# A mixing projection of eight block rows rewritten as seven block products, in a decoder block on one Trainium2 core

## The chip, the cores and the metric

One core of one Trainium2 chip runs the whole kernel in one launch. The metric is device time in microseconds (us), lower is better. Engines are named as in the profile: PE (matrix products; PEld is its weight load), DVE (vector), ACT (scalar), POOL (GpSimd), SP (the queue that issues nearly all DMAs).

## The reference, cut to what matters

```python
...
merged = jax.nn.sigmoid(z_ga) * y_attn + jax.nn.sigmoid(z_gc) * y_conv
x = x + rms_norm(merged @ w_mix_out[l], g_post_mix[l])
h = rms_norm(x, g_pre_ffn[l])
x = x + rms_norm(swiglu_ffn(h, w_ffn_in[l], w_ffn_out[l]), g_post_ffn[l])
```

Everything is float32; the change concerns `merged @ w_mix_out` and the norms behind it. `merged` has 1024 tokens by 1024 channels and `w_mix_out` is 1024 by 1024. `y_attn` and `y_conv` come from the attention and convolution branches ahead of this.

## The kernel before, in words

**Numbers.** Every float32 factor of a product is split into a high and a low part (type fp32r), and a product takes three matmuls: high·high, high·low, low·high. A split of 512 columns is one ACT cast (the high part) and one subtraction on DVE or POOL (the low part). One matmul is 128 rows by 128 columns by 512.

**Order.** All is unrolled and every engine runs its instructions in the order in which the program lists them (`manual_schedule`, line 71). Background work is a generator: `bg` (111) puts it in a list, and `tick` (121), called after every few matmuls, runs each generator one step further; `yield n` skips n ticks; `finish` (156) runs one to its end at once. So what a generator issues stands, on each engine, between the instructions that the main loop issues around that tick. SBUF has 42 tiles of 128x1024 (`slot`, line 80), 11 of 128x512 (`half`) and 3 of 128x1024 (`ring`). `B.weights(i)` (262) hands out weight tile i in split form, and has the loads and splits of the next ones issued ahead.

**The attention output projection** (1627 to 1643): for each n of 8, two units of 12 matmuls (n: 128 channels; unit: half of the tokens), then two DVE operations that multiply by a gate and add the convolution branch (1635, 1636; both have 128x512), an ACT cast (1638) and a DVE subtraction (1641): the split `merged`, transposed, in 16 tiles `mop`. POOL takes half of the weights' low parts (`wsplit`, 1626).

**The mixing projection** (1659 to 1687): tokens in tiles of 128, first two together and then one after another. For a tile, 8 channel blocks by 3 matmuls by 2 halves of the output columns accumulate into two PSUM banks (1671); 384 matmuls in all. All eight split weights stay in SBUF.

**The norms** (`mix_norm`, 1384, through `residual`, 1365) are the background of the next tile's matmuls. For one tile: two ACT squares with a sum, 128x512 from PSUM (1370); `rstd_rows` (1352), one ACT square root and five DVE operations on one column; two DVE products with gain and 1/root (1377); two DVE additions of x (1381); the store of the sum `x2` (1388). Then the second norm: an ACT square of 128x1024 (1392), `rstd_rows` again, an ACT scaling of 128x1024 to `hn` (1394). After the fourth tile of a half, 8 times four PE transposes of 128x128 (1402), an ACT scaling from PSUM (1408) and a split (1404; `split` is 1259, its ACT cast 1262, its DVE subtraction 1263): the tokens' half of `h2`, the FFN's input.

**The FFN** begins (1726 to 1738) with two columns j for the first token half, which need `h2[0]`; then the last tile's norm is finished and the same is done for the second half. Each unit calls `tick` 8 times. The norm of tile 7 and the transposes of `h2[1]` run as background of the first half. The FFN's output product (1931 to 1980) already is a product of seven block products in the form that the change gives the mixing projection.

Of the kernel before, what the change touches and what calls it, by code (L numbers as in the profile page):

```python
# [27 lines left out]
RMS_EPS = 1e-6  # L28

ROOT = 1 / 32  # L30
# [28 lines left out]
def f(ap):  # L59
    return ap.bitcast(F32)  # L60


class Build:
# [1298 lines left out]
        nc.vector.tensor_tensor(r, r, t, op=OP.mult)  # L1362
        return r

    def residual(self, banks, x, gain, out, gap=0):

        nc = self.nc
        ss = self.tiny(4, "ss", 4)
        for nh in range(2):
            nc.scalar.activation(out[:, nh * H:(nh + 1) * H], banks[nh], AF.Square, scale=ROOT, accum_out=ss[:, nh:nh + 1])  # L1370
        yield gap
        nc.vector.tensor_scalar(ss[:, 2:3], ss[:, 0:1], RMS_EPS, None, op0=OP.add)
        r = self.rstd_rows(ss[:, 1:2], ss[:, 2:3])
        yield gap
        for nh in range(2):
            s = slice(nh * H, (nh + 1) * H)
            nc.vector.scalar_tensor_tensor(out[:, s], banks[nh], r, gain[:, s], op0=OP.mult, op1=OP.mult)
            yield gap
        for nh in range(2):
            s = slice(nh * H, (nh + 1) * H)  # L1380
            nc.vector.tensor_tensor(out[:, s], out[:, s], x[nh], op=OP.add)
            yield gap

    def mix_norm(self, tt, banks, x):
        nc = self.nc
        x2 = self.ring()
        yield from self.residual(banks, x, self.g_mix, x2)
        nc.sync.dma_start(self.d_x2[tt], x2)
        yield 1
        hn = self.slot()  # L1390
        ss = self.tiny(4, "ss", 4)
        nc.scalar.activation(hn, x2, AF.Square, scale=ROOT, accum_out=ss[:, 0:1])
        r = self.rstd_rows(ss[:, 0:1], self.eps_rms)
        nc.scalar.activation(hn, x2, AF.Copy, scale=r)
        self.hn[tt // 4].append(hn)
        if tt % 4 == 3:
            yield 8
            op, y = [], None
            for kt in range(8):
                ps = self.bank("s")  # L1400
                for i in range(4):
                    nc.tensor.transpose(ps[:, i * 128:(i + 1) * 128], self.hn[tt // 4][i][:, kt * 128:(kt + 1) * 128], self.ident)
# [5 lines left out]
                nc.scalar.activation(y, ps, AF.Copy, scale=self.col(C_PREF + kt))  # L1408
                self.h2f[tt // 4].append(y)
                yield 1  # L1410
            op.append(self.split(y, H))
            self.h2[tt // 4] = op
            self.hn[tt // 4] = None

    def row_gain(self, src):
        g = self.slot()
# [4 lines left out]
def build(ctx, tc, aps):  # L1421
# [5 lines left out]
    def job(src, n=1024, kind=""):  # L1427
        J.append((src, n, kind))
        return len(J) - 1
# [18 lines left out]
    mx = [job(aps["w_mx"][j]) for j in range(8)]  # L1448
# [138 lines left out]
    def gate_load(d, late=0):  # L1587
        c = B.slot()
        if late:
            B.later(late, lambda: nc.sync.dma_start(c, d))  # L1590
        else:
            nc.sync.dma_start(c, d)
        return c

    nxt = gate_load(B.d_gc[0], 1)
    ws = {}
# [22 lines left out]
        B.finish(e)  # L1619
    if B.tags["g"] == 2:  # L1620
        B.banks(g=6, s=2)
    mop = [[None] * 8, [None] * 8]

    rest = lambda: None
    B.PIECE = 1
    B.wsplit = nc.gpsimd
    for n in range(8):

        B.ahead = int(n >= 5)
        w = B.weights(ao[n])  # L1630
        (c, y), nxt = nxt, (gate_load(B.d_ga[n + 1]), gate_load(B.d_gc[n + 1])) if n < 7 else None
        for hf in range(2):
            s = slice(hf * H, (hf + 1) * H)
            ps = B.unit(w, lambda kt: tuple(x[:, s] for x in B.OT[kt]), 4)
            nc.vector.tensor_tensor(c[:, s], ps, c[:, s], op=OP.mult)
            nc.vector.tensor_tensor(c[:, s], c[:, s], y[:, s], op=OP.add)
# [5 lines left out]
    y = None  # L1642
    rest()
    B.OT = None

    W = [B.weights(mx[0])]
    B.g_mix = B.row_gain(aps["g_mix_row"])
    B.hn, B.h2, B.h2f = [[], []], [None, None], [[], []]
    norms = []
# [7 lines left out]
    B.PIECE = 2  # L1657
    xt = {0: load_x(0), 1: load_x(1)}
    for tiles in ((0, 1), (2,), (3,), (4,), (5,), (6,), (7,)):
        banks = {tt: (B.bank(), B.bank()) for tt in tiles}  # L1660
        for kt in range(KT):
            if len(W) == kt:
                B.ahead = int(kt < KT - 1)
                W.append(B.weights(mx[kt]))
            for tt in tiles:
                m = mop[tt // 4]
                o = (tt % 4) * 128
                for st, wt, a, b in ((m[kt][:, o:o + 128], W[kt][0], 1, 0), (m[kt][:, o:o + 128], W[kt][1], 0, 0),
                                     (m[kt][:, H + o:H + o + 128], W[kt][0], 0, 1)):
                    for nh in range(2):  # L1670
                        nc.tensor.matmul(banks[tt][nh], st, wt[:, nh * H:(nh + 1) * H], start=bool(kt == 0 and a),  # L1671
                                         stop=bool(kt == KT - 1 and b))
                B.tick()
                B.tick()
            if tiles[0] == 7:
                W[kt] = None
        B.PIECE = 3
        B.ahead = 0
        m = None
        for tt in tiles:  # L1680
            if tt % 4 == 3:
                mop[tt // 4] = None
            if tt < 6:
                xt[tt + 2] = load_x(tt + 2)
            for e in norms[:-1]:
                B.finish(e)
            norms.append(B.bg(B.mix_norm(tt, banks[tt], xt.pop(tt))))
    for e in norms[:-1]:
        B.finish(e)


    B.PIECE = 4
    held = {}
# [38 lines left out]
    B.g_mix = None  # L1732
# [22 lines left out]


    NP = FT // 2
    ORDER = (("A11", "B11"), ("A12", "B21"), ("S2", "T2"), ("S1", "T1"), ("S4", "B22"), ("S3", "T3"), ("A22", "T4"))
    wo = aps["w_fo"]
    Wo, al, ws, T2, T3 = {}, {}, {}, {}, {}  # L1760
    L, R = slice(0, H), slice(H, T)

    def w_load(p, r, c):
        if (p, r) not in Wo:
# [293 lines left out]
```

## Time and profile before

| | us |
|---|---|
| median of 3 runs (lowest, highest) | 1708.28 (1707.19, 1709.27) |
| span of the profiled execution, first to last instruction | 1704.7 |
| median above that span | 3.6 |
| PE busy | 1686.8 (99%) |
| DVE, ACT, POOL busy | 1260.4 (74%), 800.6 (47%), 499.0 (29%) |
| mixing projection, first to last matmul issue | 969.1 to 1060.1 |

The profiled execution has no time of its own beside its span; the 3.6 us that the median has above it stand for what lies around the span. A row of instruction groups has: line, engine, operation, out<-in, shape, count | busy us, mean ns of one | idle time ahead of it and what ended it. A row of a timeline has: start us, duration us (of several merged ones, from the first's start to the last's end), engine, line, operation, out<-in, count [idle ahead <- what ended it]. A row of windows has: stretch, its length, then busy us and count for each engine, the granted clock, the DMA share and GB/s. Matmuls overlap in the pipeline: one lasts 0.39 us, but they follow each other faster.

### The profile page before, as it was taken

What the parts mean: (1) busy time and instruction counts of PE and PEld (TensorE: products, weight loads), DVE (VectorE), ACT (ScalarE), POOL (GpSimd) and SP (SyncE); (2) the same over time, 40 slices, a digit from 0 to 9 for tenths busy, and PEclk for the clock granted to TensorE, in tenths of its full rate; (3) what the DMA queues carried; (4) which work ended last, traced back from release to release, by engine and by line L of the source; (5) the groups of instructions that cost most, each with busy time, mean ns of one, the idle gap of its engine ahead of it and who ended that gap; (6) DMA issues with size and microseconds to landing.
All of it is one profiled execution on the core that took longest, in us unless ns stands there. A gap on an engine that the chain in (4) does not pass through costs nothing.

```text
span 1704.7 us, 23850 instructions
## 1 busy us (share of the span) xinstructions
PE 1686.8 (99%) x8374; PEld 1417.7 (83%) x8374; DVE 1260.4 (74%) x2216; ACT 800.6 (47%) x1574; POOL 499.0 (29%) x397
## 2 busy tenths in 40 slices
PE   8999999999999999999999999999999999999998
PEld 7788888888888889999888888888888888888886
DVE  6789988888999767777885845675565556677686
ACT  6344344434444576777712436633333333354463
POOL 0017777887886254655300310000000000000000
PEclk9999999999999999999999999999999999999999
DMA  4252433455567887778998722133223322494234
GB/s 166 104 185 87 149 124 130 152 196 177 173 167 176 269 266 211 222 218 224 311 290 294 254 74 88 68 111 112 93 93 112 111 93 93 155 376 137 102 133 155
DMA packets 162357, 283.39 MB, mean 166 GB/s; under 512 B 47249, under 2 KB 78732, under 8 KB 162236
## 3 DMA queue, kind: packets, MB, share of 16 engines
q1 hardware_dynamic: 161516, 281.18, 51.2%
q8 instruction: 66, 1.08, 0.3%
q0 software_dynamic: 432, 0.42, 0.1%
q14 instruction: 55, 0.45, 0.1%
q10 hardware_dynamic: 288, 0.27, 0.0%
HBM read 191.10 MB, written 95.42 MB: 168 GB/s over the span
## 4 chain that ended last, share of the span: by engine, by line
PE 94%; DMA 2%; ACT 1%; POOL 1%; issue 1%; DVE 1%; SPq 0%; DVEq 0%; ACTq 0%; POOLq 0%
PE p L334 15%; PE p L335 15%; PE p L336 15%; PE p L1942 12%; PE p L961 5%; PE p L1671 5%; PE p L318 5%; PE p L320 5%; PE p L319 5%; PE p L1142 3%; PE p L962 2%; PE p L1069 2%; PE p L569 2%; PE p L1107 2%; DMA b<-dk 1%
## 5 line engine op out<-in xcount | busy, mean ns | idle before, releaser
L334 PE MATMUL p<-b,b 128*128 128x512 f32 x1204 | 469.3, 390 | 0.5 <-ACT c L353 0.3
L335 PE MATMUL p<-b,b 128*128 128x512 f32 x1204 | 469.0, 389 | 0.0
L336 PE MATMUL p<-b,b 128*128 128x512 f32 x1204 | 468.9, 389 | 0.0
L334 PEld LDWEIGHTS p<-b,b 128*128 128x128 f32 x1204 | 226.1, 188 | 48.5 <-DVE c L853 1.0
L336 PEld LDWEIGHTS p<-b,b 128*128 128x128 f32 x1204 | 226.0, 188 | 47.0
L335 PEld LDWEIGHTS p<-b,b 128*128 128x128 f32 x1204 | 226.1, 188 | 46.8
L1942 PE MATMUL p<-b,b 128*128 128x512 f32 x924 | 209.6, 389 | 0.0
L1942 PEld LDWEIGHTS p<-b,b 128*128 128x128 f32 x924 | 173.5, 188 | 35.9
L699 DVE SCALAR_TENSOR_TENSOR p<-b,par,p 128x511 f32<-128x511 f32 (+14 forms) x232 | 163.3, 738 | 0.0
L318 PE MATMUL p<-b,b 128*128 128x512 f32 x368 | 147.3, 400 | 0.0
L961 PE MATMUL p<-b,b 128*128 128x512 f32 x384 | 145.0, 410 | 0.0
L320 PE MATMUL p<-b,b 128*128 128x512 f32 x368 | 143.8, 391 | 0.0
L319 PE MATMUL p<-b,b 128*128 128x512 f32 x368 | 143.6, 390 | 0.0
L208 ACT CAST b<-d 128x1024 fp32r<-128x1024 f32 x86 | 90.4, 1051 | 105.2 <-POOL d L229 55.1
L209 POOL TENSOR_TENSOR b<-d,b 128x1024 fp32r<-128x1024 f32 x44 | 106.9, 2430 | 79.9 <-ACT b L208 72.5
L209 DVE TENSOR_TENSOR b<-d,b 128x1024 fp32r<-128x1024 f32 x42 | 51.3, 1221 | 101.0 <-ACT b L208 101.0
L1263 DVE TENSOR_TENSOR b<-b,b 128x512 fp32r<-128x512 f32 x133 | 92.0, 696 | 23.2 <-ACT b L1262 21.2
L962 PE MATMUL p<-b,b 128*128 128x256 f32 x384 | 107.7, 281 | 0.0
L1262 ACT CAST b<-b 128x512 fp32r<-128x512 f32 x133 | 82.1, 619 | 47.6 <-PE p L1942 18.4
L1671 PE MATMUL p<-b,b 128*128 128x512 f32 x384 | 89.4, 392 | 0.0
L1082 ACT ACTIVATE c<-c,stat 128x128 f32<-128x128 f32 (+1 forms) x192 | 85.1, 447 | 6.7 <-DVE stat L1072 6.6
L208 ACT CAST b<-b 128x1024 fp32r<-128x1024 f32 x47 | 49.5, 1052 | 78.7 <-POOL b L236 37.2
(234 smaller groups left out, 2910.5 us busy)
## 6 DMA issues: line engine op xcount, KB each, us to landing
b<-w_in SPq DMA_DIRECT2D x30, 512.0 KB, 4.8
dk<-c SPq DMA_DIRECT2D x48, 256.0 KB, 3.0
dq<-c SPq DMA_DIRECT2D x48, 256.0 KB, 3.6
b<-dq SPq DMA_DIRECT2D x48, 256.0 KB, 3.9
b<-dk SPq DMA_DIRECT2D x48, 256.0 KB, 7.1
b<-w_fi SPq DMA_DIRECT2D x24, 512.0 KB, 4.7
d<-w_in SPq DMA_DIRECT2D x23, 512.0 KB, 4.1
dqS<-c SPq DMA_DIRECT2D x44, 256.0 KB, 2.1
```

What stands on the lines that cost most here:

```text
L209: self.wsplit.tensor_tensor(lo, x, f(hi), op=OP.subtract)
L318: nc.tensor.matmul(ps, hi[:, s], a, start=kt == 0, stop=False)
L319: nc.tensor.matmul(ps, hi[:, s], b, start=False, stop=False)
L320: nc.tensor.matmul(ps, lo[:, s], a, start=False, stop=kt == nk - 1)
L334: nc.tensor.matmul(ps, hi[:, s], a, start=first and kt == 0, stop=False, skip_group_check=True)
L335: nc.tensor.matmul(ps, hi[:, s], b, start=False, stop=False, skip_group_check=True)
L336: nc.tensor.matmul(ps, lo[:, s], a, start=False, stop=kt == 3, skip_group_check=True)
L699: nc.vector.scalar_tensor_tensor(A[i][:, j:], src[i][:, :H - j], w[i], A[i][:, j:], op0=OP.mult, op1=OP.add)
L961: nc.tensor.matmul(ps, a, w, start=kt == 0, stop=kt == KT - 1, skip_group_check=True)
L962: nc.tensor.matmul(ps[:, 256:], b, w[:, :256], start=False, stop=kt == KT - 1, skip_group_check=True)
L1671: nc.tensor.matmul(banks[tt][nh], st, wt[:, nh * H:(nh + 1) * H], start=bool(kt == 0 and a), stop=bool(kt == KT - 1 and b))
L1942: nc.tensor.matmul(acc[t], x, y, start=first and e == 0, stop=last and e == 2, skip_group_check=True)
```

## The change

The product `merged @ w_mix_out` is cut into 2 by 2 blocks on each side (token half and channel half; channel half and output half) and computed by seven block products in place of eight, with sums of blocks ahead of them and sums of results behind them (Winograd's form of Strassen's scheme). A block product is 4 channel blocks (p) by 4 token tiles (t) by 3 matmuls; each result has four PSUM banks, one for each t; the banks of X and Y are accumulated over several products and copied to SBUF in between (`C`).

- The weights `w_mx` are no longer split jobs: each is loaded whole (`Wm`) in the attention output projection's loop, one for each n.
- `merged` stays unsplit (`M`). `parts` issues, five steps ahead of the matmuls, the operands of step k (28 steps: 7 products by 4 p): `merged_part` (cast, DVE split, DVE sums) and `mixing_part` (ACT cast, POOL split, POOL sums).
- The order is A11·B11, A12·B21, S2·T2, S1·T1, S4·B22, S3·T3, A22·T4. Of the first token half the right output columns end in the fifth product, of the second half in the sixth and the left ones in the seventh.
- The sum of squares is made in two halves of the columns (`part_norm`), a half each time that one is complete; the gain is multiplied there too. `mix_norm` then has the rest. In the fifth product t is the outer loop, and each token tile's norm starts as that tile ends. The last two products alternate by token tile.

```diff
+    ORDER = (("A11", "B11"), ("A12", "B21"), ("S2", "T2"), ("S1", "T1"), ("S4", "B22"), ("S3", "T3"), ("A22", "T4"))
+    def merged_part(k):
...
+        al[k] = B.split(x, H)
+        if name == "A11":
+            add(half_of(S3, p), a[:, L], a[:, R], op=OP.subtract)
+        elif name == "A12":
+            add(a[:, R], a[:, R], b[:, R], op=OP.add)
+            add(a[:, L], a[:, R], a[:, L], op=OP.subtract)
+            add(b[:, L], b[:, L], a[:, L], op=OP.subtract)
...
+    def mixing_part(k):
+        sub = nc.gpsimd.tensor_tensor
...
+        if name == "T2":
+            sub(x, Wm[p, 1][:, R], Wm[p, 0][:, L], op=OP.subtract)
+        s = B.slot(F32R)
+        nc.scalar.copy(s[:, L], x)
+        sub(s[:, R], x, f(s[:, L]), op=OP.subtract)
...
+        if name == "B21":
+            sub(y[:, L], y[:, R], y[:, L], op=OP.subtract)
+        elif name == "T1":
+            sub(half_of(T2, p), Wm[p, 1][:, L], half_of(T2, p), op=OP.subtract)
+        elif name == "B22":
+            sub(T3[p][:, R], Wm.pop((p, 1))[:, R], T3[p][:, R], op=OP.subtract)
...
     for n in range(8):
+        Wm[p, r] = B.slot()
+        nc.sync.dma_start(Wm[p, r], aps["w_mx"][2 * p + r])
...
-            x = B.slot(F32R)
-            nc.scalar.copy(x[:, :H], c[:, s])
-            mop[hf][n] = x
-            rest()
-            rest = lambda x=x, c=c[:, s]: nc.vector.tensor_tensor(x[:, H:], c, f(x[:, :H]), op=OP.subtract)
+        M[n] = c
+        if n % 2 and n > 1:
+            parts(n // 2)
...
+    def part_norm(h, t, c, src):
+        nc.scalar.activation(B.junk(), src, AF.Square, scale=ROOT, accum_out=SM[h][t][:, c:c + 1])
+        nc.vector.tensor_tensor(o, src, B.g_mix[:, (L, R)[c]], op=OP.mult)
...
+    parts(4)
+    for i in range(4):
...
+        for p in range(NM):
+            for t in range(4):
+                mm(acc[t], t, k, p == 0 and i in (0, 1, 3), p == NM - 1)
+                if t == 0:
+                    parts(k + 5)
+        if i == 0:
+            for t in range(4):
+                nc.scalar.copy(C[0][t][:, L], X[t])
+        elif i == 1:
+            bg.append(B.bg(left0(Y)))
...
+    for t in range(4):
+        for p in range(NM):
+            mm(Y[t], t, k, False, p == NM - 1)
+            if p == 0:
+                parts(k + 5 + t)
+        nc.vector.tensor_tensor(o, Y[t], o, op=OP.add)
+        part_norm(0, t, 1, o)
+        for e in norms[:-1]:
+            B.finish(e)
+        norms.append(B.bg(tile_norm(0, t, 1)))
...
+    parts(7 * NM)
+    for i, t in ((5, 0), (5, 1), (6, 0), (5, 2), (6, 1), (5, 3), (6, 2), (6, 3)):
+        for p in range(NM):
+            mm(X[t], t, i * NM + p, False, p == NM - 1)
+        if i == 5:
+            nc.vector.tensor_tensor(o, X[t], o, op=OP.add)
+            part_norm(1, t, 1, o)
+        else:
+            part_norm(1, t, 0, X[t])
+            for e in norms[:-1]:
+                B.finish(e)
+            norms.append(B.bg(tile_norm(1, t, 0)))
```

In the diff the first loop over p runs the first four products (i from 0 to 3; `left0` adds and `part_norm`s the first half's left columns), the loop over t the fifth, and the list of pairs (i, t) the last two: i = 5 completes the second half's right columns, i = 6 its left ones and with them the tile.

In `mix_norm` two DVE operations (product with 1/root, sum with x, in one) take the place of the four at lines 1377 and 1381; its steps are: nothing, `rstd_rows`, the two DVE operations and the store, one tick skipped, the second norm, and for the fourth tile of a half eight ticks skipped ahead of the transposes.

More of the change, by code (lines that the diff above doesn't have):

```diff
@@ L1363, in rstd_rows, with junk, mix_norm @@
         return r
-    def residual(self, banks, x, gain, out, gap=0):
+    def junk(self):
+        return self.half()
+    def mix_norm(self, h, t, C, sums, c, x):
         nc = self.nc
[L1368 to L1374, printed above, removed]
+        yield 0
+        o, C[t] = C[t], None
+        r = self.rstd_rows(sums[:, c:c + 1], sums[:, 2:3])
+        yield 0
+        x2 = self.ring()
         for nh in range(2):
             s = slice(nh * H, (nh + 1) * H)
[L1377 to L1387, printed above, removed]
+            nc.vector.scalar_tensor_tensor(x2[:, s], o[:, s], r, x[nh], op0=OP.mult, op1=OP.add)
+        tt = 4 * h + t
         nc.sync.dma_start(self.d_x2[tt], x2)
+        o = x = None
         yield 1
@@ L1624, in build, with parts @@
+    done = 0
+    def parts(upto):
+        nonlocal done
+        while done < min(upto, 7 * NM):
+            merged_part(done)
+            mixing_part(done)
+            done += 1
     rest = lambda: None
@@ L1626, in build @@
     B.wsplit = nc.gpsimd
+    B.banks(g=6, s=2)
     for n in range(8):
@@ L1655, in load_x @@
         return x
[L1657 to L1684, printed above, removed]
@@ new lines, in tile_norm, with left0, mm @@
+    def tile_norm(h, t, c):
+        yield from B.mix_norm(h, t, C[h], SM[h][t], c, xt.pop(4 * h + t))
+    def left0(Y):
+        for t in range(4):
+            o = C[0][t][:, L]
+            nc.vector.tensor_tensor(o, Y[t], o, op=OP.add)
+            part_norm(0, t, 0, o)
+            first_half(0, t, 0)
+            yield 2
+    def mm(bank, t, k, first, last):
+        a, w = al[k], ws[k]
+        h, l = a[:, t * 128:(t + 1) * 128], a[:, H + t * 128:H + (t + 1) * 128]
+        for x, y, e in ((h, w[:, L], 0), (h, w[:, R], 1), (l, w[:, L], 2)):
+            nc.tensor.matmul(bank, x, y, start=first and e == 0, stop=last and e == 2, skip_group_check=True)
+        B.tick()
@@ L1685, in build @@
             for e in norms[:-1]:
                 B.finish(e)
-            norms.append(B.bg(B.mix_norm(tt, banks[tt], xt.pop(tt))))
+            norms.append(B.bg(tile_norm(1, t, 0)))
+            if t < 2:
+                xt[6 + t] = load_x(6 + t)
+        if t == 3:
+            for p in range(NM):
+                del al[i * NM + p], ws[i * NM + p]
+    o = X = None
     for e in norms[:-1]:
@@ L1757, in build @@
     NP = FT // 2
[L1758 removed]
     wo = aps["w_fo"]
[L1760 to L1761 removed]
+    Wo, T2, T3 = {}, {}, {}
     def w_load(p, r, c):
```

94 lines of the change are left out of this document (81 added, 13 removed).

## The prediction, made before the result was known

> **What bounds the kernel now.** First the page's head and three rows of its instruction groups:
>
> ```profile
> PE 1686.8 (99%) x8374; PEld 1417.7 (83%) x8374; DVE 1260.4 (74%) x2216; ACT 800.6 (47%) x1574; POOL 499.0 (29%) x397
> ...
> L1942 PE MATMUL p<-b,b 128*128 128x512 f32 x924 | 209.6, 389 | 0.0
> ...
> L1671 PE MATMUL p<-b,b 128*128 128x512 f32 x384 | 89.4, 392 | 0.0
> ...
> L348 ACT COPY c<-p 128x512 f32<-128x512 f32 x43 | 25.3, 589 | 112.8 <-PE p L336 102.0 <-issue 8.9 <-ACT c L858 2.0
> ```
>
> PE is busy 99% of the span. A matmul is shown as 389 ns long, but they follow each other: 209.6 / 924 = 0.227 us each is the price of one more or one less. Next the mixing stage alone: the matmuls by their source line, the waits of PE from 926 to 1110 us, and the busy time of the stage.
>
> ```profile
> L1671 PE MATMUL p<-b,b x384: 386/390/479, 969.1 to 1060.1; 128*128 128x512 f32 x192
> ```
>
> ```profile
> PE p L1402 <- ACT b L1408: 0.2, 1, 0.2
> ```
>
> ```profile
> 969.00:1060.00 91.00, 90.81 (x417) 74.99 (x416) 51.70 (x128) 49.04 (x98) 11.52 (x7) 1.00 0.33 119
> ```
>
> From the first matmul to the end of the last are 91.2 us: 384 x 0.227 = 87.1, and 4.1 for the 32 transposes of the first token half. PE waits 0.2 us in 184 us. The stage's columns after PE and PEld are DVE 51.7, ACT 49.0 and POOL 11.5 us of 91. So here PE is the bound, and a matmul saved is time saved as long as the others keep up.
>
> They are not free to do so. One tile's norm, on ACT and then on DVE:
>
> ```profile
> 1016.98 0.30 ACT L1357 ACTIVATE rr<-ss 128x1 f32<-128x1 f32 x1
> 1020.85 1.06 ACT L1392 ACTIVATE b<-d 128x1024 f32<-128x1024 f32 x1 [3.57 <-DVE d L1381]
> ...
> 1022.03 0.29 ACT L1357 ACTIVATE rr<-ss,eps_rms 128x1 f32<-128x1 f32 x1
> 1023.19 1.15 ACT L1394 ACTIVATE b<-d,rr 128x1024 f32<-128x1024 f32 x1 [0.86 <-DVE rr L1362]
> 1024.25 0.58 ACT L1370 ACTIVATE d<-p 128x512 f32<-128x512 f32 x1
> ```
>
> ```profile
> 1018.14 1.41 DVE L1377 SCALAR_TENSOR_TENSOR d<-p,rr,b 128x512 f32<-128x512 f32 x2
> 1019.47 1.28 DVE L1381 TENSOR_TENSOR d<-d,c 128x512 f32<-128x512 f32 x2
> ```
>
> ACT and DVE hand the tile to and fro, each idle while the other works, and both keep their program's order, so the next tile's work waits behind it. A tile takes 8 to 9 us, hidden beside 10.9 us of PE (48 matmuls). The last one ends here:
>
> ```profile
> 1070.07 1.15 ACT L1394 ACTIVATE b<-d,rr 128x1024 f32<-128x1024 f32 x1 [0.87 <-DVE rr L1362]
> 1071.13 1.12 ACT L190 CAST b<-b 128x512 fp32r<-128x512 f32 x2
> 1073.20 0.69 ACT L1408 ACTIVATE b<-p,par 128x512 f32<-128x512 f32 x1 [0.95 <-PE p L1402]
> ```
>
> Tile 7's `hn` is there at 1071.2; PE comes to its transposes 18 ticks into the FFN, 1060.3 + 18 x 3 x 0.227 = 1072.5. There is 1.3 us to spare.
>
> **Term 1, matmuls: -10.9 us.** 7 x 4 x 4 x 3 = 336 instead of 384; 48 x 0.227 = 10.9. A step (k, four token tiles) takes 12 x 0.227 = 2.72 us. The transposes stay.
>
> **Term 2, operands: +12 us (0 to 17).** Before, 16 + 16 casts, 24 DVE and 8 POOL subtractions made the operands. Now it is 56 casts, 28 + 16 on DVE (splits and sums), 28 + 16 on POOL, all 128x512 and nearly all with two inputs in SBUF. Rows of POOL and DVE at the end of the attention projection, where they meet:
>
> ```profile
> 962.01 1.29 POOL L191 TENSOR_TENSOR b<-b,b 128x512 fp32r<-128x512 f32 x1 [4.54 <-PE p L320]
> ```
>
> ```profile
> 962.00 0.68 DVE L1635 TENSOR_TENSOR b<-p,b 128x512 f32<-128x512 f32 x1
> 962.72 1.13 DVE L1636 TENSOR_TENSOR b<-b,b 128x512 f32<-128x512 f32 x1
> ```
>
> ```profile
> 973.26 11.52 POOL L191 TENSOR_TENSOR b<-b,b 128x512 fp32r<-128x512 f32 x7 [4.37 <-ACT b L190]
> ```
>
> ```profile
> 973.74 9.90 DVE L191 TENSOR_TENSOR b<-b,b 128x512 fp32r<-128x512 f32 x6 [0.32 <-issue]
> ```
>
> The DVE operation with an input in PSUM (out<-in `b<-p,b`) runs in its usual 0.68 beside POOL; the one with two SBUF inputs at 962.72 ends 0.55 after POOL has ended at 963.30. With both queues full they alternate, 9.90 / 6 to 11.52 / 7 = 1.65, at full contention 1.7 us for a pair; alone DVE has one each 0.6 (1019.47 above: two in 1.28) and POOL one each 1.3.
>
> Count time from the first mixing matmul. DVE comes out of the attention projection at 1.4 and has four operations for steps 2 and 3, then four for each of steps 4 to 7 (A12: split and three sums); POOL has two for each of these. Alternating, step 4's split is ready at 10.2 (due at 10.9), step 5's, the ninth, at 17.2 (due 13.6), and the next two come 4.6 us apart instead of 2.72, since S2·T2 keeps POOL going: waits of 3.6, 1.9, 1.9, and 1.9 at step 8, together 9.2. Then DVE has one split a step and gets ahead, and POOL is next: 15 operations from step 12 to the split of step 19, from 36.6 on, with ACT's casts in between held behind `left0`'s squares. That gives step 19 at about 60, where PE would be at 54.8: 5.1 more, 14.3 in all. If some of POOL's work can begin before the attention projection ends (its tiles might be free), up to three operations, 3.6 us, come off; I take 12. Lower end 0: POOL alone, 31 operations to that point x 1.29 = 40, fits into the 45.6 us before step 19. Upper end 17: all of them and 36 DVE operations x 0.6 one after another from 1.4 on make 63, against 45.6.
>
> Edits at nothing: the 12 copies of results to SBUF (0.59, L348's row) hold ACT until a product ends, with casts queued behind that are due five steps, 13.6 us, later; without this lead each would cost up to its wait. The fifth product writes banks just copied, as the FFN's output does at L1942, which is in no row of PE's waits. The `w_mx` loads move ahead in SP's queue, past gate loads; five to six free PSUM banks keep PE going there, and if that fails it is one landing:
>
> ```profile
> b<-w_mx SPq DMA_DIRECT2D x8, 512.0 KB, 3.2
> ```
>
> **Term 3, norms: +34 us (7 to 44).** A tile of the first token half is now complete only in the fifth product, one of the second in the seventh. So all eight norms start behind Z, the end of the fifth product's first tile (43.5 + 2.7 = 46.2, plus term 2), where before the first two started after 21 us. From Z on PE has three more tiles, 8.2, the last two products, 21.8, 32 transposes, 4.1, and 14 ticks of the FFN, 9.5, until it comes to tile 7's transposes (the generator's steps are fewer now, 14 ticks in place of 18): 43.6 us.
>
> What ACT and DVE do one after another in that time, in program order: for a tile a square 0.7, from square root to product 1.16 (1016.98 to 1018.14), two products 1.33 (1018.14 to 1019.47), the next tile's addition 0.65, the second norm 3.40 (1020.85 to 1024.25), together 7.24; the next tile's square stands behind its addition, and that behind this tile's products, so tiles do not overlap. 8 x 7.24 = 57.9. Between them stand the casts of steps 21 to 27, four more squares (2.8), the table load at the first square root, and the copies and casts of `h2[0]`:
>
> ```profile
> 972.00 7.39 ACT L190 CAST b<-b 128x512 fp32r<-128x512 f32 x14
> ```
>
> ```profile
> 992.12 1.28 ACT L1357 ACT_TABLE_LOAD   x1
> ```
>
> ```profile
> 1036.20 0.62 ACT L1262 CAST b<-b 128x512 fp32r<-128x512 f32 x1
> 1036.72 0.68 ACT L1408 ACTIVATE b<-p,par 128x512 f32<-128x512 f32 x1
> 1037.44 0.62 ACT L1262 CAST b<-b 128x512 fp32r<-128x512 f32 x1
> ```
>
> 14 casts 7.4, the load 1.3, 8 x 1.24 = 9.9. Sum 79; following the queues instruction by instruction, some 1.5 of it lie side by side: 77.8. So PE waits 77.8 - 43.6 = 34.2, in pieces: for step 23's operands, cast behind two norms (about 11), steps 24 to 27 (5), the first transposes of `h2[0]` (6), and the transposes of `h2[1]` in the FFN (13). Behind that the second half's splits are as far ahead of the FFN's need as before. Lower end: ACT's own work without any waiting, 12 squares 8.4, 8 x 2.9, casts 7.4, `h2[0]` 9.9, load 1.3, is 50.2, so 6.6. Upper end: nine POOL operations, 1.1 each, also stand in the way of the products: 44. I take the walk, since the rows show tiles strictly one after another.
>
> **Sum**, against the median of 1708.3 (3.6 above the profiled span of 1704.7, and nothing outside the span changes): -10.9 + 12 + 34.2 = +35.3, **1743.6 us**.
>
> **Rivals.** (a) *The ports cost nothing*: POOL runs far enough ahead, and only the norms decide: 1708.3 - 10.9 + 34.2 = 1731.6. For it: POOL's weights depend on loads alone. Against it: the 1.7 us pairs. (b) *PE stays the bound*, the faster side: the norms of successive tiles overlap on ACT and DVE. The other work in the chain is 77.8 - 57.9 = 19.9, so it is worth the whole 10.9 (1697.4) if a tile takes up to (43.6 - 19.9) / 8 = 3.0 us, and nothing from (54.5 - 19.9) / 8 = 4.3 us, against 7.24 in the rows; for it, ACT's own share of a tile is only 2.9 + 0.7. (c) *Only the ports cost*: norms hidden as in (b), 1708.3 - 10.9 + 12 = 1709.4, no change to be seen. (d) *PE comes back slow after each wait*. The start of the trace, where PE had idled 6 us:
>
> ```profile
> 0.00:10.00 10.00, 3.96 (x9) 2.82 (x10) 2.96 (x9) 5.34 (x9) 2.16 (x12) 1.00 0.75 273
> 10.00:20.00 10.00, 10.00 (x46) 8.24 (x45) 7.06 (x9) 7.88 (x13) 0.00 (x0) 1.00 1.03 413
> ```
>
> Nine matmuls took 3.96 us there, later ones 10 / 46 = 0.22 each, so such a restart loses 3.96 - 9 x 0.227 = 1.9; part may be data, since first operands were just arriving. Most of my waits are set by other engines and swallow it; two restarts that count (step 19, the FFN) give +3.8: 1747.4. [...]
>
> **Chances.** Forecast (both terms) 0.52; (a) 0.22; (d) 0.10; (b) 0.11; (c) 0.05. The range holds the forecast, (a) and (d): down to (a) with a third of the chain's 34 overlapped, 1731.6 - 11.4 = 1720, up to both upper prices, 1708.3 - 10.9 + 17 + 44 = 1758. A difference of 0.2%, 3.4 us, is about what a measurement of this kernel tells from no change: faster 0.11, within it 0.05, slower 0.84.
>
> **What would show it.** Term 1: 336 matmuls in the mixing lines. Term 2: PE waits on DVE or POOL at products two, three and five, and DVE splits there that last up to 1.7 us. Term 3: ACT idling on DVE, and PE on ACT, at steps 23 to 27 and at both groups of transposes; tile 7's `hn` some 25 to 40 us later than before, counted from the first mixing matmul (102.1 before). It is wrong if PE's waits in the stage stay under 10 us, or if tiles' second norms follow each other at under 4.3 us.

## The result and the profile after

| | before | after |
|---|---|---|
| median, us | 1708.35 | 1754.1 (1753.45 to 1758.94) |
| ratio to before | | 1.0275 [1.0259, 1.0291], slower |
| span of the profiled execution | 1704.7 | 1757.1 |
| first mixing matmul | 969.1 | 974.4 |

The change costs 45.7 us; 1743.6 had been forecast, with a range up to 1758. The profiled execution is the longest of the four, 1758.94; a run's time is 1.8 us above its span here, where 3.6 had been taken from the median before and one profiled span. Its mixing projection begins 5.3 us later than in the profile before. In experiments 4, 6 and 11, whose code is the same up to there, it begins at 969.3 to 970.0, and in all the profiles shown here anywhere from 968.5 to 974.4, so this is the execution's and not the change's. As in the prediction, all is counted from the first mixing matmul, called s0.

The page's head, the row of the mixing matmuls (idle time of PE ahead of them in the last part), and the row of windows over the stage (length; PE, PEld, DVE, ACT, POOL busy; clock):

```profile
PE 1695.7 (97%) x8326; PEld 1417.2 (81%) x8326; DVE 1308.3 (74%) x2247; ACT 817.1 (46%) x1608; POOL 554.8 (32%) x434
...
L1749 PE MATMUL p<-b,b 128*128 128x512 f32 x336 | 93.4, 437 | 34.4 <-DVE b L1804 15.2
```

```profile
974.40:1107.70 133.30, 96.00 (x369) 73.53 (x368) 99.59 (x157) 69.03 (x137) 63.00 (x41) 0.83 0.17 58
```

336 matmuls instead of 384, as meant, in a stage of 133.3 us instead of 91.2; PE is idle in it for 37, and the granted clock, 1.00 before, is 0.83. Where PE waits is in its timeline, in order (rows with a wait of over 1.1 us; in brackets the wait and who ended it):

```profile
991.15 7.71 PE L1749 MATMUL p<-b,b 128*128 128x512 f32 x24 [2.50 <-DVE b L1263]
1000.43 3.01 PE L1749 MATMUL p<-b,b 128*128 128x512 f32 x12 [1.57 <-DVE b L1263]
1005.15 12.77 PE L1749 MATMUL p<-b,b 128*128 128x512 f32 x55 [1.71 <-DVE b L1263]
...
1032.00 1.32 PE L1749 MATMUL p<-b,b 128*128 128x512 f32 x3 [1.93 <-POOL b L1659]
1034.46 12.48 PE L1749 MATMUL p<-b,b 128*128 128x512 f32 x44 [1.15 <-POOL b L1659]
...
1057.20 0.79 PE L1749 MATMUL p<-b,b 128*128 128x512 f32 x1 [6.88 <-ACT b L1658]
...
1074.64 6.95 PE L1749 MATMUL p<-b,b 128*128 128x512 f32 x18 [10.49 <-DVE b L1804]
1091.76 0.66 PE L1396 MATMUL p<-ident,b 128*128 128x128 f32 x4 [2.93 <-ACT b L1402]
...
1102.60 5.28 PE L1749 MATMUL p<-b,b 128*128 128x512 f32 x12 [4.73 <-DVE b L1804]
1119.78 0.33 PE L1396 MATMUL p<-ident,b 128*128 128x128 f32 x1 [2.03 <-ACT b L1387]
```

The first three are low parts of `merged` (L1263 is `split`'s subtraction), the next two low parts of weights on POOL (L1659), 1057.20 the cast of step 23's weights. 1074.64 and 1102.60 wait for L1804, VectorE's addition that reads the sixth product's result from PSUM: the seventh product accumulates in that bank, so it can't begin before the read. The last row is tile 7's `hn` (L1387), 14 ticks into the FFN.

Where does a norm's time go? One tile of the fifth product, on ACT and on DVE (start, duration):

```profile
1042.73 0.63 ACT L1727 ACTIVATE c<-b 128x512 f32<-128x512 f32 x1 [2.92 <-DVE b L1788]
...
1043.36 1.04 ACT L1385 ACTIVATE b<-d 128x1024 f32<-128x1024 f32 x1
...
1045.69 1.15 ACT L1387 ACTIVATE b<-d,rr 128x1024 f32<-128x1024 f32 x1 [0.87 <-DVE rr L1362]
1046.74 0.60 ACT L1262 CAST b<-b 128x512 fp32r<-128x512 f32 x1
1047.25 0.61 ACT L1658 CAST b<-b 128x512 fp32r<-128x512 f32 x1
1047.77 0.29 ACT L1357 ACTIVATE rr<-so 128x1 f32<-128x1 f32 x1
1052.01 0.63 ACT L1727 ACTIVATE c<-b 128x512 f32<-128x512 f32 x1 [3.96 <-DVE b L1788]
...
1061.30 0.63 ACT L1727 ACTIVATE c<-b 128x512 f32<-128x512 f32 x1 [3.96 <-DVE b L1788]
```

```profile
1042.01 0.68 DVE L1788 TENSOR_TENSOR b<-p,b 128x512 f32<-128x512 f32 x1
1043.48 0.69 DVE L1729 TENSOR_TENSOR b<-b,b 128x512 f32<-128x512 f32 x1 [0.79 <-ACT c L1727]
1044.52 0.16 DVE L1358 TENSOR_TENSOR rr<-ss,eps_rms 128x1 f32<-128x1 f32 x1 [0.35 <-ACT b L1385]
...
1047.37 0.69 DVE L1263 TENSOR_TENSOR b<-b,b 128x512 fp32r<-128x512 f32 x1 [1.72 <-ACT b L1262]
1047.98 1.24 DVE L1358 TENSOR_TENSOR rr<-so 128x1 f32<-128x1 f32 x1
...
1049.97 1.41 DVE L1378 SCALAR_TENSOR_TENSOR d<-b,rr,c 128x512 f32<-128x512 f32 x2
1051.30 0.68 DVE L1788 TENSOR_TENSOR b<-p,b 128x512 f32<-128x512 f32 x1
```

The square of one tile follows that of the tile before after 9.28 and 9.29 us. DVE waits for ACT at the gain product (0.79), at the second root (0.35) and at the operand's split (1.72); ACT waits for DVE 3.96 a tile ahead of the next square alone. In the first of these 9.28 us DVE is busy for 6.0 and ACT for 4.4, and nothing of the next tile comes between.

### The profile page after: what moved, and what is told of

Read it like the earlier page. It is cut to its first block, busy times and chain, and to the rows that moved or that the text cites. A ratio compares the mean times of both kernels' runs of the same rounds, so it can differ in the third digit from the quotient of the medians.

```text
span 1757.1 us, 23834 instructions
## 1 busy us (share of the span) xinstructions
PE 1695.7 (97%) x8326; PEld 1417.2 (81%) x8326; DVE 1308.3 (74%) x2247; ACT 817.1 (46%) x1608; POOL 554.8 (32%) x434
## 5 line engine op out<-in xcount | busy, mean ns | idle before, releaser
L334 PEld LDWEIGHTS p<-b,b 128*128 128x128 f32 x1204 | 226.0, 188 | 49.0 <-DVE c L853 1.0
L335 PEld LDWEIGHTS p<-b,b 128*128 128x128 f32 x1204 | 226.0, 188 | 46.8
L336 PEld LDWEIGHTS p<-b,b 128*128 128x128 f32 x1204 | 226.0, 188 | 46.7
L2070 PEld LDWEIGHTS p<-b,b 128*128 128x128 f32 x924 | 173.3, 188 | 37.3 <-DVE c L1979 1.2
L1263 DVE TENSOR_TENSOR b<-b,b 128x512 fp32r<-128x512 f32 x161 | 124.2, 779 | 34.1 <-ACT b L1262 31.1
L1262 ACT CAST b<-b 128x512 fp32r<-128x512 f32 x161 | 99.4, 619 | 71.3 <-PE p L2070 20.4
L1749 PE MATMUL p<-b,b 128*128 128x512 f32 x336 | 93.4, 437 | 34.4 <-DVE b L1804 15.2
L1749 PEld LDWEIGHTS p<-b,b 128*128 128x128 f32 x336 | 69.9, 213 | 56.0 <-issue 10.9
```

Of the source, the lines that this page charges most:

```text
L334: nc.tensor.matmul(ps, hi[:, s], a, start=first and kt == 0, stop=False, skip_group_check=True)
L335: nc.tensor.matmul(ps, hi[:, s], b, start=False, stop=False, skip_group_check=True)
L336: nc.tensor.matmul(ps, lo[:, s], a, start=False, stop=kt == 3, skip_group_check=True)
L1263: nc.vector.tensor_tensor(s[:, 512:512 + n], src, f(s[:, :n]), op=OP.subtract)
L1749: nc.tensor.matmul(bank, x, y, start=first and e == 0, stop=last and e == 2, skip_group_check=True)
L2070: nc.tensor.matmul(acc[t], x, y, start=first and e == 0, stop=last and e == 2, skip_group_check=True)
```

## The experiments

My theory: two things cost. The operands come late, since DVE and POOL alternate (term 2), and the norms start late and run tile after tile (term 3). The rivals: one of the two alone, PE coming back slowly after waits, or VectorE short of time as such. Differences are against the kernel after, 1754.1; each interval is of the ratio to the kernel before on the same chip, whose medians there are 1707.1 to 1708.5.

**1. All subtractions on VectorE.** In `mixing_part`:

```diff
-        sub = nc.gpsimd.tensor_tensor
+        sub = nc.vector.tensor_tensor
```

> The weights' subtractions and sums of the mixing projection (44 of 128x512) go from POOL to DVE; the result is the same. Theory (two separate costs: some 15 us because DVE and POOL keep each other from SBUF, some 40 us because the norms' chain on ACT and DVE runs one tile after another): a pair no longer costs 1.7 us but two DVE operations at 0.6, 67 of them up to step 19 are 40 us of the 45.6 there, so PE's waits ahead of the fifth product fall from about 15 to 0 to 4; behind it the small DVE operations no longer wait for POOL (-4) and eight more splits stand on DVE (+5). About 1741, between 1737 and 1746. Rival (the port is the whole of it, the norms come late only because the operands do): about 1705. Rival (DVE is simply short of time): slower than 1754.

Measured: 1750.2, ratio 1.0239 [1.0219, 1.0259]. Only 3.9 came off, much less than expected. The waits for L1263 are gone, but in their place stands a row that the kernel after has with 0.9 only, the wait for `left0`'s addition:

```profile
PE p L1749 <- DVE b L1740: 5.7, 3, 3.0
```

Without the alternation VectorE has every operation itself, and its additions come late. So it is not the alternation alone.

**2 and 3. Mixing norms without their squares and roots**, the root replaced by 1; then the same with edit 1 on top:

```diff
-        r = self.rstd_rows(sums[:, c:c + 1], sums[:, 2:3])
...
-        nc.scalar.activation(hn, x2, AF.Square, scale=ROOT, accum_out=ss[:, 0:1])
-        r = self.rstd_rows(ss[:, 0:1], self.eps_rms)
-        nc.scalar.activation(hn, x2, AF.Copy, scale=r)
+        nc.scalar.activation(hn, x2, AF.Copy, scale=1.0)
...
-        nc.scalar.activation(B.junk(), src, AF.Square, scale=ROOT, accum_out=SM[h][t][:, c:c + 1])
```

> Leaves out of the mixing projection's norms the squares and the reciprocal roots (the products with gain, the sum with x, one scaling copy on ACT and the transposes stay), so the result is not normalised there; POOL stays as in the change. Theory: without the passing to and fro a tile costs DVE two products and an addition, ACT one copy, and PE's waits behind the fifth product's first tile fall from about 40 us to under 6; the 15 us ahead of it stay or fall a little, since the casts no longer stand behind left0's squares. About 1717, between 1710 and 1723. Rival (port alone): no faster than 1745.

> Both of the above: subtractions and sums on DVE, no squares and no roots in the mixing projection's norms. Theory: both covers of the gain are gone, and the 48 matmuls saved (10.9 us) show: about 1700, between 1696 and 1706. If a third cost is hidden in the change (loads moved ahead, the copies of results, PE coming back slowly), it stays above 1706.

Measured: 1726.0 (1.0097 [1.0079, 1.0116]) and 1717.1 (1.0051 [1.0032, 1.0069]). The squares and roots are worth 28 us, the largest single part. With both edits 1700 was expected (at most 1706); PE's waits there name what I had not counted:

```profile
PE p L1744 <- DVE b L1799: 7.4, 2, 5.7
...
PE p L1744 <- DVE b L1735: 4.2, 2, 2.2
```

(L1799 is the addition that reads the sixth product's bank, L1735 `left0`'s.) Even without roots VectorE comes late to read results. So there is a third thing, its queue.

**4. The fifth product's operands ahead of its norms:**

```diff
-            if p == 0:
-                parts(k + 5 + t)
+            if t == 0:
+                parts(k + 5)
```

> In the fifth product the operands of steps 20 to 23 are issued beside its first token tile instead of one beside each tile, so that they do not stand behind the norms of the first two tiles; nothing else changes. Theory (the chain of norms as a whole is what PE waits for): PE's waits of about 18 us for steps 21 to 23 go, but the same time is waited later, at the transposes; only the casts that no longer stand in the chain, some 3 us, are gained: about 1751, between 1748 and 1754. Rival (the order is the fault: operands queued behind norms): the waits at these steps are gained in full, 1736 to 1743.

Measured: 1753.5, ratio 1.0264 [1.0242, 1.0286]: no change, as the theory had it. The wait for step 23 is gone, and the next one has taken it all:

```profile
PE p L1749 <- DVE b L1804: 26.8, 2, 22.1
```

Which instruction PE waits for is a matter of order; how long, of the chain behind it.

**5. Norms two tiles at a time**, with one root on two columns and the second tile's products beside the first one's square:

```diff
+        r = self.root_pair(sums[:, 2 * c:2 * c + 2], sums[:, 4:6])
...
+        for j in range(2):
...
+                nc.vector.scalar_tensor_tensor(x2[:, s], o[:, s], r[:, j:j + 1], xs[j][nh], op0=OP.mult, op1=OP.add)
...
+            nc.scalar.activation(hn, x2, AF.Square, scale=ROOT, accum_out=ss[:, j:j + 1])
...
+        r = self.root_pair(ss[:, 0:2], None)
```

> The eight norms go two tiles at a time: one root on two columns for both tiles, so eight handovers between ACT and DVE in place of sixteen, and the square of the first tile beside the products of the second. Theory (the norms cost because ACT and DVE wait for each other, tile after tile): of the 28 us that taking the roots out brought, about 20 come off: 1734 us (1726 to 1742); tiles follow each other at under 6 us instead of 9.3, and the longest wait for the read of the sixth product's bank shrinks below 6 us. Rival (VectorE has simply too much to do, and the roots count by their operations): 80 small operations become 48, 32 x 0.16 = 5 us: 1749 (1746 to 1752).

Measured: 1745.5, ratio 1.0220 [1.0204, 1.0235]: 8.6 off, between theory and rival and less than half of what I expected; the longest wait for the read of the sixth product's bank is still 7.4. From Z (the end of the fifth product's first tile) to the last `hn` are now 75.7 us instead of 84.0. Within a pair the two engines still stand and wait, ACT 2.5 us for the first product of each pair and DVE for each square, so pairing halves the handovers and not the chain.

**6. The fifth product's sum left in PSUM**, so that square and gain product read it side by side:

```diff
-        o = C[0][t][:, R]
-        nc.vector.tensor_tensor(o, Y[t], o, op=OP.add)
+        o = Y[t]
+        nc.vector.tensor_tensor(o, o, C[0][t][:, R], op=OP.add)
```

> In the fifth product the sum of the two halves is left in its PSUM bank, so that ScalarE's square and VectorE's product with the gain read it side by side and the product no longer overwrites what the square reads. Theory (the handover adds 0.8 us to each of the first half's four tiles, one of the reasons why a tile takes 9.3 us and not 8.3): 4 x 0.8 = 3.2 us off, 1751 (1749.5 to 1752.5). Rival (the 0.8 us is taken out of a wait that the tile has anyway): 1754 (1753 to 1755.5).

Measured: 1753.2, ratio 1.0264 [1.0248, 1.0279]: the 0.9 can't be told from none, and the theory falls. In the kernel with all three edits (8, below), which has this one too, DVE still waits 0.75 for the square, though the product no longer writes over anything:

```profile
1029.43 0.69 DVE L1795 TENSOR_TENSOR b<-p,b 128x512 f32<-128x512 f32 x1 [0.75 <-ACT c L1793]
```

So the edit doesn't take the wait away there. Nor would it have helped: in the rows of the kernel after, the gain product is done at 1044.17 (1043.48 + 0.69), and DVE's next operation, the second root, has to wait until 1044.52 for ACT anyway. The 0.79 lies beside the chain and not on it.

**7. Operands spread**: VectorE subtracts for the first four products' weights, POOL for the rest, and A12's third sum is made one product later.

```diff
+        elif name == "S2":
             add(b[:, L], b[:, L], a[:, L], op=OP.subtract)
...
-        sub = nc.gpsimd.tensor_tensor
+        sub = (nc.vector if k < 16 else nc.gpsimd).tensor_tensor
```

> The weights' operands of the first four products are subtracted on VectorE, those of the last three on GpSimd, and the third sum of each A12 block is made one product later. Theory (the early waits come from the two engines alternating, and the later ones from VectorE's backlog, so a spread load takes most of the 15 us): waits in the first four products under 2 us and those at steps 18 and 19 gone, 1744 (1740 to 1748), below the 1750.2 of the kernel with all subtractions on VectorE. Rival (what is gained early is waited for again in the norms, which set the end anyway): 1750 (1748 to 1754).

Measured: 1750.9, ratio 1.0250 [1.0232, 1.0267], 3.2 below the kernel after, with overlapping intervals. The rival: Z is 59.4 us behind s0 instead of 61.3, and PE waits 6.4 for `left0`'s additions, as in experiment 1.

**8. The edits 5, 6 and 7 together.**

> The three edits together: norms in pairs, the fifth product's sum left in PSUM, operands spread. Theory (they take away different things): the sum of the three, 1754 - 20 - 3 - 10 = 1721 (1710 to 1732), still slower than the kernel before. Faster than before (under 1705) only if the pairs alone bring the chain under PE's time there, the 1697 of the matmuls saved being the floor. Rival (VectorE's total work is what counts in the end): over 1735.

Measured: 1742.1, ratio 1.0197 [1.0182, 1.0212]. 12.0 off, about the sum of what the three brought (8.6 + 0.9 + 3.2 = 12.7), as if they took away different things, but far from the 33 that I had put on them: the time lies where the rival had it, over 1735.

**9. On top of 8, another order**: operands of the last two products ahead of the norms, the sixth product's reads ahead of the next pair, `h2[1]`'s transposes 12 ticks later.

```diff
-            if p == 0:
-                parts(k + 5 + t)
+            if t < 2:
+                parts(21 + 4 * t + p)
...
-    for i, t in ((5, 0), (5, 1), (6, 0), (5, 2), (6, 1), (5, 3), (6, 2), (6, 3)):
+    for i, t in ((5, 0), (5, 1), (6, 0), (6, 1), (5, 2), (5, 3), (6, 2), (6, 3)):
...
+        yield from tile_norm(1, 2, 0)
+        yield 18
+        yield from B.mix_transposes(1)
```

> On top of the three edits together: operands of the last two products ahead of the norms, VectorE's reads of the sixth product's banks ahead of the next pair of norms, and the second half's transposes some 12 ticks (8 us) later in the FFN. Theory (tensor engine waits because reads and operands stand behind norms in the queues, and the norms themselves have cover left in the FFN): 1742 less about 12, 1730 (1720 to 1737), the waits for the sixth product's read from 12.5 us to under 5. Rival (only the sum of the chain counts, as in the run with the operands first): waits move to the transposes, 1742 (1738 to 1746).

Measured: 1742.1, ratio 1.0196 [1.0178, 1.0214]; the rival. The longest wait for the sixth product's read grew to 12.4 (7.5 in 8), and the last `hn` comes 136.2 us behind s0 (133.0 in 8). Nor does other cover help: here too the order chooses the wait and not the time.

**10. No mixing norms at all**, operands spread as in 7. `mix_norm` keeps the store and a copy:

```diff
+        nc.sync.dma_start(self.d_x2[4 * h + t], o)
...
+        nc.scalar.copy(hn, o)
...
-        nc.scalar.activation(B.junk(), src, AF.Square, scale=ROOT, accum_out=SM[h][t][:, c:c + 1])
```

> The mixing norms are left out whole (no squares, roots, gains, residual products; the sum is stored and copied as it is), with the operands spread over both engines. Theory (the norms started late are all that is left of the loss, and the matmuls saved are worth 48 x 0.227 us): 1697.4 to 1701, 7 to 11 us under the kernel before. Rival (something else in the seven products costs too, the reads of the sixth product's banks or the copies): 1704 to 1710.

Measured: 1707.6, ratio 1.0001 [0.9991, 1.0010]. The norms are worth 43.2 (from 1750.9), but this is the kernel before, not 10 us under it: the rival. PE's rows with a wait:

```profile
1002.22 4.15 PE L1739 MATMUL p<-b,b 128*128 128x512 f32 x17 [0.23 <-DVE b L1650]
1007.63 0.97 PE L1739 MATMUL p<-b,b 128*128 128x512 f32 x3 [1.26 <-DVE b L1730]
1010.03 25.46 PE L1739 MATMUL p<-b,b 128*128 128x512 f32 x111 [1.44 <-DVE b L1730]
1037.98 5.28 PE L1739 MATMUL p<-b,b 128*128 128x512 f32 x15 [2.49 <-DVE b L1794]
...
1057.41 3.06 PE L1739 MATMUL p<-b,b 128*128 128x512 f32 x12 [0.33 <-DVE b L1794]
```

The stage is 89.0 us long, 2.2 less than before (s0 came 2.3 later in this execution, which makes up for it). So 8.7 of the 10.9 saved are lost in it. In it are 5.8 us of waits for VectorE, and one loss beside them: the 15 matmuls at 1037.98 take 5.12 us to the next instruction's start at 1043.10 (the first transposes) instead of 15 x 0.227 = 3.41, so 1.7 more. Together 7.5 of the 8.7.

**11. PE kept busy through its two waits for the sixth product's read:**

```diff
+        n = {(6, 0): 44, (6, 3): 20}.get((i, t), 0)
...
+            for e in range(n):
+                nc.tensor.matmul(o, al[i * NM][:, :128], ws[i * NM][:, L], start=e == 0, stop=e == n - 1)
```

> The changed kernel with 44 and 20 matmuls into an unused bank put into its two waits for the sixth product's read (10.5 and 4.7 us), so that TensorE works on through them. Theory (the chain on ACT and DVE sets the end, so slow matmuls behind a wait are hidden by the next wait; the chain itself waits for TensorE under 3 us): 1753.5 (1751 to 1756), while the granted clock behind those waits is 1.00 in place of 0.6 to 0.8. Rival (TensorE coming back slowly is part of the loss): 4 to 8 us off, 1746 to 1750.

Measured: 1750.8, ratio 1.0251 [1.0231, 1.0272], 3.3 below the kernel after and just between the two expectations; the intervals overlap. The clock behind the waits did rise. The windows after the first wait (kernel after, then this kernel):

```profile
1074.60:1088.90 14.30, 14.19 (x64) 11.57 (x64) 8.19 (x25) 8.56 (x19) 0.00 (x0) 0.80 0.41 137
```

```profile
1070.00:1084.00 14.00, 11.10 (x63) 9.18 (x61) 8.82 (x28) 9.87 (x22) 0.00 (x0) 1.00 0.43 139
```

64 matmuls and transposes kept PE busy for 14.2 us, 63 now for 11.1: 3 us sooner, and PE then waits 3.17 at the transposes instead of 2.93. From Z to the last `hn` are 81.7 us instead of 84.0. So the chain sets the end, and a slow PE costs there what the chain itself waits for PE, at most some 3 us.

**12. Matmuls alone.** As 10, with the first product's four pairs of operands used for all seven:

```diff
-        while done < min(upto, 7 * NM):
+        while done < min(upto, NM):
...
-        a, w = al[k], ws[k]
+        a, w = al[k % NM], ws[k % NM]
```

> The mixing norms are left out, and so are the operands of the last six products: all seven products use the first one's four pairs of operands, so that ACT, DVE and GpSimd make 4 steps of operands instead of 28. Matmuls, copies, sums of results and banks are those of the changed kernel. Theory (48 matmuls at 0.227 us are worth 10.9 us; the run without norms got none of it because the operands keep VectorE full): TensorE waits under 1 us in the stage and 1697.4 (1695.5 to 1699.5), 10.9 under the kernel before. Rival (copies, sums of results and the handing on of banks cost by themselves): waits for the sixth product's read stay, 1702 to 1708.

Measured: 1698.1, ratio 0.9951 [0.9937, 0.9965]. The only row in which PE waits in this stage, and the stage's windows row:

```profile
PE p L1739 <- DVE b L1794: 0.3, 1, 0.3
```

```profile
969.00:1058.00 89.00, 88.71 (x407) 73.40 (x406) 20.10 (x30) 30.19 (x44) 0.00 (x0) 1.00 0.30 103
```

From s0 (969.7) to the FFN's first matmul (1050.1) are 80.4 us, against 91.2 before. So copies of results, banks and reads cost nothing by themselves, and the read of the sixth product's bank, which made PE wait 2.5 us in 10, is late only when operands have to be made.

**In four steps**: matmuls saved -9.0 (12 against before); operands +9.5 (10 against 12); norms +43.2 (7 against 10); operands unspread +3.2 (after against 7). Together +46.9, where 45.7 were measured. That they add up proves nothing, since each is the difference to the next kernel; the 1.2 lies between two medians of the kernel before, 1708.35 and 1707.14. The intervals are 2 to 3 us to either side, and in another order the steps can come out otherwise: the price of the operands was measured without norms, that of the norms with the operands spread. No version that computes the whole came out ahead of the kernel before.

## Why the prediction was right, and where it was not

Slower by 35.3 was forecast, and 45.7 came; direction and mechanism hold, and two terms were too small. In the profiled execution, 145.4 us pass from s0 (974.43) to the transposes of tile 7 (1119.78); before, it was 91.2 and 14 ticks, 9.5, to that place in the FFN: 100.7. The 44.6 more divide like this:

- **Term 1, matmuls: -10.9.** Right. Experiment 12 has 10.8 in the stage and 9.0 in the whole.
- **Term 2, operands: +12 forecast, 15.1 measured.** VectorE's first addition of the fifth product, which waits for PE only, starts at 1035.72, 61.3 behind s0; 46.2 had been worked out for that point without term 2 (experiment 12 has 46.5). 

```profile
1035.72 0.69 DVE L1788 TENSOR_TENSOR b<-p,b 128x512 f32<-128x512 f32 x1 [0.76 <-PE p L1749]
```

  The mechanism is the one foreseen, one pair of operations every 1.70 us:

```profile
979.73 1.74 POOL L1663 TENSOR_TENSOR b<-b 128x512 f32<-128x512 f32 x1
981.43 1.74 POOL L1659 TENSOR_TENSOR b<-b,b 128x512 fp32r<-128x512 f32 x1
```

```profile
978.54 1.78 DVE L1636 TENSOR_TENSOR b<-b 128x512 f32<-128x512 f32 x1
980.24 1.77 DVE L1263 TENSOR_TENSOR b<-b,b 128x512 fp32r<-128x512 f32 x1
981.94 1.78 DVE L1636 TENSOR_TENSOR b<-b 128x512 f32<-128x512 f32 x1
```

  Counted on PE, the early waits are 5.8 (9.2 in the walk) and the late ones, at steps 18 and 19, 3.1 (5.1), with 0.9 for `left0` between. The other 5.3 are matmuls that follow each other more slowly behind these waits, which the term had left out: the 24 at 991.15 take 7.7 us instead of 5.4, at a granted clock of 0.56 in their first 3.9 us. Yet it is POOL that sets Z, and there the walk holds. It had POOL begin fifteen operations at 36.6 and end step 19's at about 60; these are the first and the last of the fifteen, from 36.0 to 60.0 behind s0:

```profile
1010.47 1.43 POOL L1659 TENSOR_TENSOR b<-b,b 128x512 fp32r<-128x512 f32 x1 [3.62 <-PE p L1749]
...
1033.14 1.27 POOL L1659 TENSOR_TENSOR b<-b,b 128x512 fp32r<-128x512 f32 x1
```

  What was wrong in the term is the 2.3 taken off the walk's 14.3 for POOL work begun early: POOL stands idle for 3.62 just ahead of these fifteen, so work begun earlier would hardly have brought them forward. That removing the alternation brings only 3.9 (experiment 1) I had not seen: VectorE then lacks the time itself.
- **Term 3, norms: +34.2 forecast, 40.4 measured.** The last `hn` ends at 1118.6 + 1.15, 84.0 behind Z, where 77.8 had been counted. Counted from s0 it comes 43.2 later than before, just over the 25 to 40 named as a sign:

```profile
L1387 ACT ACTIVATE b<-d,rr x8: 1147/1148/1154, 1045.7 to 1118.6; 128x1024 f32<-128x1024 f32 x8
```

  The step that failed is the tile's 7.24 us, 8.3 with the two casts of a step: the second, third and fourth tile follow each other at 9.28. Followed through the rows above, the second tile takes 0.72 for the addition, 0.63 square, 1.16 second square, 1.17 root, 1.05 scaling, 1.03 casts, 2.20 from square root to products (1047.77 to 1049.97) and 1.33 for these. All but one are as the prediction had them; the one is the root, 2.20 in place of 1.16, because its first operation takes 1.24 instead of 0.16 while POOL subtracts. The third tile's root loses the same 1.04; one more stands behind splits as well and takes 3.02 from square root to scaling (1067.25 to 1070.27) in place of 1.17, so these three lose 3.9 of the 6.2 by which the chain is longer than counted. Beside the first tile's root POOL works too, but the table load on ACT, 1.28 us from 1038.22 on, hides it, and no other is touched. ACT's two waits for PE, 0.89 and 1.30, which the walk put at nothing, are about the rest; in experiment 11 no square waits for PE, and there `hn` comes 2.3 sooner behind Z:

```profile
1067.25 0.29 ACT L1357 ACTIVATE rr<-ss,eps_rms 128x1 f32<-128x1 f32 x1
1070.27 1.15 ACT L1387 ACTIVATE b<-d,rr 128x1024 f32<-128x1024 f32 x1 [2.73 <-DVE rr L1362]
...
1080.13 0.60 ACT L1727 ACTIVATE c<-p 128x512 f32<-128x512 f32 x1 [0.89 <-PE p L1749]
...
1082.12 0.69 ACT L1402 ACTIVATE b<-p,par 128x512 f32<-128x512 f32 x1 [1.30 <-PE p L1396]
```

  POOL's part had been kept for the upper end ("nine POOL operations, 1.1 each"); three of them belonged into the sum. Experiments 2 and 10 fit the size of the term: roots and squares 28 us, all of the norms 43.
- **Where PE waits** was wrong in its largest piece. I had put 11 on step 23's operands (7.4 measured with 0.55 for its subtraction), 5 on steps 24 to 27, 6 and 13 on the two groups of transposes (2.9 and 2.0). In truth 15.2 fall on the seventh product's wait for the sixth's bank to be read, a dependence that I had read over in the order of the last two products. It didn't spoil the sum, since the chain sets it (experiments 4 and 9).
- **Rivals.** (a), *the ports cost nothing*, is out with the pairs of 1.70 us and a Z that comes 15.1 late; but operands cost 9.5 even when spread, and no run parts the alternation from VectorE's time, or shows what makes the two engines alternate; "the ports" was my name for it. (b), PE stays the bound, would have needed tiles at 3.0 us. (c), only the ports, is what is left when the norms are gone: experiment 10 gives 1707.6, and 1709.4 was worked out for it, though with operands not spread, so the closeness is in part chance. (d), PE's slow return, is real but mostly hidden: of the 145.4, 89.8 are work (76.2 of matmuls, 4.1 of transposes, 9.5 of FFN) and 39.2 waits (35.9 in the rows shown, 3.3 in four smaller ones), so 16.4 are matmuls that follow each other at more than 0.227 us. Those ahead of Z run into the next wait for DVE or POOL; keeping PE at work through its two waits for L1804 gave 3.3 at most. No run keeps PE busy at the other waits.

What stays open: 2.4 us behind the mixing projection in the profiled execution, of which a wait of 0.8 on an addition in the FFN's output product, not there before, is one part; and why the gain product in experiment 8, with the edit of 6, waits 0.75 for a square that reads the same bank.

## What to carry to other kernels

Saving matmuls pays only where the engines that make the operands and take the results have time to spare in that same stage; here 10.9 us of PE were bought with 9.5 us of operands. Ask of a reordered product when its first complete result appears: all that hangs on results (here eight norms) moves behind that point, and a chain that hands over between two engines costs whatever it is longer than the work left to cover it (here 84.0 against 43.6). When a wait is taken away and the next one grows by as much, look for the chain and not for the next order.

## What the runs showed of the hardware

- **Behind waits of 2.5 us the granted clock was lower.** Behind 2.49 us of waiting (experiment 10) PE was granted this:

```profile
1037.90:1041.50 3.60, 3.52 (x11) 2.87 (x12) 0.53 (x1) 0.00 (x0) 0.00 (x0) 0.69 0.02 5
```

  11 matmuls in 3.5 us, 0.32 each instead of 0.227. In the kernel after it is 0.56 over 3.9 us behind the wait of 2.50, and 1.00 behind those of 1.57 and 1.71, but 0.64 over the 1.4 us behind that of 1.93. Where waits follow each other, it is 0.60 over 17 us:

```profile
1047.00:1064.20 17.20, 7.96 (x18) 4.96 (x18) 12.38 (x27) 8.39 (x19) 3.61 (x3) 0.60 0.33 112
```

  Beside the slow start of the trace before (nine matmuls in 3.96 us) the column stands at 1.00; in these stages it goes down with PE's pace. How long a wait has to be for that, and how long the lower clock lasts, no run was made to show.
- **A one-column operation took 1.24 us beside POOL.** VectorE's first operation of a root, 128x1, took 1.24 us beside the one below; in twelve of the kernel's sixteen roots in this stage it took 0.15 or 0.16:

```profile
1047.94 1.27 POOL L1659 TENSOR_TENSOR b<-b,b 128x512 fp32r<-128x512 f32 x1 [8.30 <-ACT b L1658]
```

  It ends at 1049.22 (1047.98 + 1.24), POOL's at 1049.21. The other three slow ones, of 1.21 to 1.24 us, also end within 0.02 us of an operation on POOL. What holds them back the rows do not show.
